# Grouped instance norm on one core: loads and stores on one queue, in a fixed order

## The chip, the cores and the metric

The kernel runs on one core of a Trainium2 chip. The metric is the device time of one execution in microseconds (us); lower is better. Engines are named as in the profile: PE (TensorE), DVE (VectorE), ACT (ScalarE), POOL (GpSimd) and SP (SyncE). The last computes nothing here; it issues DMAs. Sixteen DMA engines carry all transfers of the core.

## The reference

Each of 4 x 8 x 16 = 512 channels, an image of 256 x 256 float32 numbers, is normalized by its own mean and variance and scaled by one number per channel.

```python
def reference(x, gamma):               # x: (4, 8, 16, 256, 256), gamma: (8, 16), float32
    mu = x.mean(axis=(3, 4), keepdims=True)
    var = ((x - mu) ** 2).mean(axis=(3, 4), keepdims=True)
    x_norm = (x - mu) / np.sqrt(var + 1e-5)
    out = x_norm * gamma[None, :, :, None, None]
    return out.astype(np.float32)
```

The input has 134.22 MB and so has the output. Each number is read once and written once.

## The kernel before

The channels are worked off in 18 units, in order. A big unit is 32 channels, each spread over 4 partitions: a tile of 128 x 16384 float32, 8.39 MB. A small unit is 16 channels, each over 8 partitions: 128 x 8192, 4.19 MB. Units 0 and 1 are small, 2 to 15 are big, 16 and 17 are small again. Three slots in SBUF of 8.39 MB hold the data (`slots`, `SLOTS = 3`). Each big unit has a slot of its own, two small ones share one, and slots are taken in turn: units 0 and 1 in slot 0, unit 2 in slot 1, unit 3 in slot 2, unit 4 in slot 0, and so on, so that big unit u takes the slot of unit u-3. Units 16 and 17 are the halves of slot 0, after unit 13.

The instructions of each engine stand in the order in which the program writes them. For a unit u they are:

- DVE sums each partition's row (L128), ACT squares it and sums the squares (L130, in pieces of 8192 numbers, two for a big unit).
- PE adds the partial sums over the partitions of a channel (L138), which gives minus the mean and minus the mean square.
- DVE, ACT and DVE turn these into a scale per partition (L141 to L156).
- DVE subtracts the mean and multiplies by the scale, in place (L159).
- ACT issues the store of the unit (L163), so the store waits in ACT's order for L159.

The loads are all issued by SP (`load`, L70). Loads 0 to 3 go out at the start. Load 4 is written after store 1, and load u+3 after store u from there on. A load into a slot waits until the store that last read the slot has landed; this wait stands on SP, the store on ACT, and so the two kinds of transfer go through two queues.

```python
        nc.scalar.dma_start(out=rows(flat_o, u), in_=t)
        if u == 1:
            load(4)
        elif 2 <= u and u + 3 < U - 1:
            load(u + 3)
            if u + 3 == U - 2:
                load(U - 1)
```

Of the kernel before, what the change touches and what calls it, by code (L numbers as in the profile page):

```python
# [1 line left out]

# [4 lines left out]

F32 = mybir.dt.float32
U8 = mybir.dt.uint8
ALU = mybir.AluOpType  # L10
ACTF = mybir.ActivationFunctionType
AX = mybir.AxisListType


@with_exitstack
def kernel(
    ctx: ExitStack,
    tc: tile.TileContext,
    x: bass.AP,
    gamma: bass.AP,  # L20
    out: bass.AP,
):
    nc = tc.nc
    B, G, C, H, W = x.shape
    P = nc.NUM_PARTITIONS
    HW = H * W
    n_ch = B * G * C
    GC = G * C
    SLOTS = 3
    FS = HW // 8  # L30
    FB = HW // 4
    KB, KS = P // 4, P // 8


    flat_x = x.rearrange("b g c h w -> (b g c h w)")
    flat_o = out.rearrange("b g c h w -> (b g c h w)")

    data = ctx.enter_context(tc.tile_pool(name="data", bufs=1))
    singles = ctx.enter_context(tc.tile_pool(name="singles", bufs=1))
    psum = ctx.enter_context(tc.tile_pool(name="psum", bufs=4, space=bass.MemoryType.PSUM))  # L40
    ctx.enter_context(tc.manual_schedule())

    slots = [data.tile([P, FB], F32, name=f"xt{i}") for i in range(SLOTS)]

    units = []
    first = 0
    turn = 0

    def small(pair):
        nonlocal first, turn  # L50
        for h in range(2):
            units.append((first, 8, slots[turn % SLOTS][:, h * FS : (h + 1) * FS]))
            first += KS
        turn += 1

    small(0)
    while first < n_ch - KB:
        units.append((first, 4, slots[turn % SLOTS][:]))
        first += KB
        turn += 1  # L60
    small(1)
    U = len(units)

    def rows(flat, u):
        c0, s, _ = units[u]
        f = HW // s
        return flat[c0 * HW : c0 * HW + P * f].rearrange("(p f) -> p f", f=f)

    def load(u):
        nc.sync.dma_start(out=units[u][2], in_=rows(flat_x, u))  # L70

    g_kn = singles.tile([KB, GC // KB], F32, name="g_kn")
    for u in range(4):
        load(u)
    with nc.allow_non_contiguous_dma(reason="128 numbers"):
        nc.gpsimd.dma_start(out=g_kn[:], in_=gamma.rearrange("g c -> (g c)").rearrange("(n k) -> k n", k=KB))  # L76

    eps_t = singles.tile([P, 1], F32, name="eps_t")
    nc.gpsimd.memset(eps_t[:], 1e-5)
    root_eps = singles.tile([P, 1], F32, name="root_eps")  # L80
    nc.scalar.activation(out=root_eps[:], in_=eps_t[:], func=ACTF.Sqrt)  # L81

    def blocks(name, rows_, k, s, value, base):

        t = singles.tile([rows_, k, P // k], F32, name=name)
        nc.gpsimd.memset(t[:], value)
        nc.gpsimd.affine_select(  # L87
            out=t[:], in_=t[:], pattern=[[-s, k], [0, P // k]], compare_op=ALU.is_ge,
            fill=0.0, base=-base, channel_multiplier=1,
        )  # L90
        nc.gpsimd.affine_select(  # L91
            out=t[:], in_=t[:], pattern=[[s, k], [0, P // k]], compare_op=ALU.is_ge,
            fill=0.0, base=s - 1 + base, channel_multiplier=-1,
        )
        return t[:].rearrange("p k s -> p (k s)")

    navg = {8: blocks("navg8", P, KS, 8, -1.0 / HW, 0), 4: blocks("navg4", P, KB, 4, -1.0 / HW, 0)}
    pick = [
        blocks("pick8a", KB, KS, 1, 1.0, 0),
        blocks("pick8b", KB, KS, 1, 1.0, KS),  # L100
        blocks("pick4", KB, KB, 1, 1.0, 0),
    ]
    NB = GC // KB
    g_ps = psum.tile([P, 3, NB], F32, name="g_ps", bufs=1)
    g_col = singles.tile([P, 3, NB], F32, name="g_col")
    for i in range(3):
        nc.tensor.matmul(out=g_ps[:, i], lhsT=pick[i], rhs=g_kn[:], start=True, stop=True)  # L107
    nc.vector.tensor_copy(out=g_col[:], in_=g_ps[:])  # L108

    def gamma_of(u):  # L110
        c0, s, _ = units[u]
        n, rest = divmod(c0 % GC, KB)
        i = 2 if s == 4 else rest // KS
        return g_col[:, i, n : n + 1]

    junk = singles.tile([P, FS], U8, name="junk")
    st = singles.tile([P, U, 3], F32, name="st")
    nvar = singles.tile([P, U], F32, name="nvar")
    rest = singles.tile([P, U], F32, name="rest")
    std = singles.tile([P, U], F32, name="std")  # L120
    rstd = singles.tile([P, U], F32, name="rstd")
    scale = singles.tile([P, U], F32, name="scale")

    before = None
    for u in range(U):
        c0, s, t = units[u]
        parts = 8 // s
        nc.vector.reduce_sum(out=st[:, u, 0:1], in_=t, axis=AX.X)  # L128
        for h in range(parts):
            square = nc.scalar.activation(  # L130
                out=junk[:], in_=t[:, h * FS : (h + 1) * FS], func=ACTF.Square,
                accum_out=st[:, u, 1 + h : 2 + h],
            )
            if h == 0 and before is not None:
                tc.declare_no_dep(square.ins, before.ins, reason="junk, ordered by the root between")
            before = square
        ps = psum.tile([P, 3], F32, name="ps")
        nc.tensor.matmul(  # L138
            out=ps[:, : 1 + parts], lhsT=navg[s], rhs=st[:, u, : 1 + parts], start=True, stop=True,
        )  # L140
        nc.vector.tensor_scalar(  # L141
            out=nvar[:, u : u + 1], in0=ps[:, 0:1], scalar1=ps[:, 0:1],
            scalar2=ps[:, 1:2], op0=ALU.mult, op1=ALU.add,
        )
        bias = eps_t[:]
        if parts == 2:
            bias = rest[:, u : u + 1]
            nc.vector.tensor_scalar(  # L148
                out=bias, in0=ps[:, 2:3], scalar1=-1.0, scalar2=1e-5, op0=ALU.mult, op1=ALU.add,
            )  # L150
        nc.scalar.activation(  # L151
            out=std[:, u : u + 1], in_=nvar[:, u : u + 1], func=ACTF.Sqrt,
            bias=bias, scale=-1.0,
        )
        nc.vector.reciprocal(out=rstd[:, u : u + 1], in_=std[:, u : u + 1])  # L155
        nc.vector.tensor_mul(  # L156
            out=scale[:, u : u + 1], in0=rstd[:, u : u + 1], in1=gamma_of(u),
        )
        nc.vector.tensor_scalar(  # L159
            out=t, in0=t, scalar1=ps[:, 0:1], scalar2=scale[:, u : u + 1],  # L160
            op0=ALU.add, op1=ALU.mult,
        )
        nc.scalar.dma_start(out=rows(flat_o, u), in_=t)  # L163
        if u == 1:
            load(4)
        elif 2 <= u and u + 3 < U - 1:
            load(u + 3)
            if u + 3 == U - 2:
                load(U - 1)


# [1 line left out]
_INS = ['x', 'gamma']  # L173
_OUTS = [((4, 8, 16, 256, 256), 'float32')]


# [23 lines left out]
```

## Time and profile before

| what | value |
|---|---|
| median of 3 runs | 631.54 us (629.13 to 643.01) |
| the profiled execution's own time | 629.47 us |
| its span in the profile | 627.8 us |
| DVE busy | 429.4 us (68%) |
| ACT busy | 234.7 us (37%) |
| loads, q1 on SP | 134.22 MB, 49.8% of the 16 DMA engines |
| stores, q10 on ACT | 134.22 MB, 49.4% |
| HBM traffic over the span | 428 GB/s |
| big load, median from issue to landing | 43.5 us |
| big store, median from issue to landing | 44.7 us |

The span is the stretch of the device's time that the profile covers; the execution's own time has 1.7 us around it. "L128" is a line of the kernel file. A row of a group gives the engine, the operation, what it writes and reads, the count, its busy time with the mean of one in ns, and the idle time before it with what ended that. The share of a queue is the time that its packets took, as a part of the span of all 16 DMA engines.

### The profile page before, as it was taken

How to read it: one execution, taken by the hardware profiler on the slowest of the kernel's cores; microseconds unless marked ns; L12 is line 12 of the kernel's file. 1: busy time of each engine (PE TensorE's matmuls, PEld its weight loads, DVE VectorE, ACT ScalarE, POOL GpSimd, SP SyncE). 2: the span in 40 equal slices, each digit the busy share in tenths (PEclk: the TensorE clock that was granted, in tenths of full speed). 3: DMA queues.
4: the chain of work that ended last, by engine and by line, in shares of the span. 5: the costliest groups of instructions: out<-in, count | busy, mean ns of one | idle time of the engine just before them, and what ended most of it. 6: DMA issues, size and time to landing. Idle time of an engine off the chain costs nothing.

```text
span 627.8 us, 434 instructions
## 1 busy us (share of the span) xinstructions
PE 11.4 (2%) x42; PEld 10.4 (2%) x42; DVE 429.4 (68%) x105; ACT 234.7 (37%) x84; POOL 6.2 (1%) x21
## 2 busy tenths in 40 slices
PE   0000000000000000000000000000000000000000
PEld 0000000000000000000000000000000000000000
DVE  1978897097692956929569395792948839499780
ACT  2438190090621706217062260712608135081340
POOL 3000000000000000000000000000000000000000
DMA  9999999999999999999999999999999999999997
GB/s 363 438 401 451 411 457 418 451 418 451 418 447 422 447 422 447 414 451 418 451 418 451 413 455 413 455 405 464 401 468 401 468 401 468 401 447 420 449 411 303
DMA packets 5218, 268.45 MB, mean 428 GB/s; under 512 B 608, under 2 KB 608, under 8 KB 608
## 3 DMA queue, kind: packets, MB, share of 16 engines
q1 hardware_dynamic: 2592, 134.22, 49.8%
q10 hardware_dynamic: 2592, 134.22, 49.4%
q14 instruction: 2, 0.02, 0.0%
q0 software_dynamic: 32, 0.00, 0.0%
HBM read 134.22 MB, written 134.22 MB: 428 GB/s over the span
## 4 chain that ended last, share of the span: by engine, by line
DMA 63%; DVE 26%; another core or an unknown queue 7%; PE 1%; issue 0%; ACT 0%; SPq 0%
DMA xt<-in_x_dram 36%; DMA out_dram<-xt 28%; DVE st L128 16%; DVE xt L159 8%; PE ps L138 1%; ACT std L151 0%; DVE nvar L141 0%; SPq L70 0%; DVE rstd L155 0%; DVE scale L156 0%; DVE rest L148 0%
## 5 line engine op out<-in xcount | busy, mean ns | idle before, releaser
L128 DVE TENSOR_REDUCE st<-xt 128x1 f32<-128x16384 f32 (+1 forms) x18 | 275.8, 15323 | 151.5 <-DMA xt<-in_x_dram 151.5
L130 ACT ACTIVATE junk<-xt 128x8192 uint8<-128x8192 f32 x32 | 224.9, 7030 | 305.6 <-DMA xt<-in_x_dram 290.0
L159 DVE TENSOR_SCALAR xt<-xt,ps,scale 128x16384 f32<-128x16384 f32 (+1 forms) x18 | 141.7, 7870 | 0.7
L151 ACT ACTIVATE std<-nvar,rest 128x1 f32<-128x1 f32 x14 | 4.1, 294 | 57.0 <-DVE rest L148 57.0
L138 PE MATMUL ps<-st,navg 128*128 128x3 f32 (+1 forms) x36 | 10.0, 349 | 586.4 <-DVE st L128 586.4
L138 PEld LDWEIGHTS ps<-st,navg 128*128 128x128 f32 x36 | 9.0, 311 | 587.4 <-issue 587.4
L141 DVE TENSOR_SCALAR nvar<-ps 128x1 f32<-128x1 f32 x18 | 5.2, 287 | 13.4 <-PE ps L138 13.4
L108 DVE COPY g_col<-g_ps 128x12 f32<-128x12 f32 x1 | 0.2, 170 | 10.6 <-PE g_ps L107 10.6
L155 DVE RECIPROCAL rstd<-std 128x1 f32<-128x1 f32 x18 | 3.0, 164 | 6.5 <-ACT std L151 6.5
L130 ACT ACTIVATION_READ_ACCUMULATOR junk<-xt 128x1 f32 x32 | 6.0, 186 | 0.0
L151 ACT ACTIVATE std<-nvar,eps_t 128x1 f32<-128x1 f32 x4 | 1.2, 294 | 9.5 <-DVE nvar L141 9.5
L156 DVE TENSOR_TENSOR scale<-rstd,g_col 128x1 f32<-128x1 f32 x18 | 2.9, 159 | 0.6
L148 DVE TENSOR_SCALAR rest<-ps 128x1 f32<-128x1 f32 x14 | 2.1, 148 | 0.0
L81 ACT ACT_TABLE_LOAD x1 | 1.3, 1283 | 0.8 <-PEq L184 0.8
L87 POOL TENSOR_SCALAR_AFFINE_SELECT navg<-navg 128x128 f32<-128x128 f32 x2 | 0.9, 468 | 0.1
L91 POOL TENSOR_SCALAR_AFFINE_SELECT navg<-navg 128x128 f32<-128x128 f32 x2 | 0.9, 458 | 0.1
L107 PE MATMUL g_ps<-g_kn,pick8a 32*128 32x4 f32 x2 | 0.6, 344 | 9.1 <-DMA g_kn<-in_gamma_dram 9.1
L76 POOL DMA_DIRECT2D g_kn<-in_gamma_dram x1 | 0.7, 671 | 0.8 <-POOLq L184 0.8
L107 PEld LDWEIGHTS g_ps<-g_kn,pick8a 32*128 32x128 f32 x2 | 0.5, 305 | 9.1 <-issue 9.1
L107 PE MATMUL g_ps<-g_kn,pick 32*128 32x4 f32 x2 | 0.6, 349 | 0.0
L107 PE MATMUL g_ps<-g_kn,pick8b 32*128 32x4 f32 x2 | 0.6, 349 | 0.0
L107 PEld LDWEIGHTS g_ps<-g_kn,pick8b 32*128 32x128 f32 x2 | 0.5, 328 | 0.0
(17 smaller groups left out, 4.9 us busy)
## 6 DMA issues: line engine op xcount, KB each, us to landing
xt<-in_x_dram SPq DMA_DIRECT2D x4, 4096.0 KB, 26.8
out_dram<-xt ACTq DMA_DIRECT2D x4, 4096.0 KB, 28.4
xt<-in_x_dram SPq DMA_DIRECT2D x14, 43.5
out_dram<-xt ACTq DMA_DIRECT2D x14, 44.7
g_kn<-in_gamma_dram POOLq DMA_DIRECT2D x1, 0.5 KB, 7.6
```

What stands on the lines that cost most here:

```text
L81: nc.scalar.activation(out=root_eps[:], in_=eps_t[:], func=ACTF.Sqrt)
L87: nc.gpsimd.affine_select(out=t[:], in_=t[:], pattern=[[-s, k], [0, P // k]], compare_op=ALU.is_ge, fill=0.0, base=-base, channel_multipli ...
L107: nc.tensor.matmul(out=g_ps[:, i], lhsT=pick[i], rhs=g_kn[:], start=True, stop=True)
L128: nc.vector.reduce_sum(out=st[:, u, 0:1], in_=t, axis=AX.X)
L130: square = nc.scalar.activation(out=junk[:], in_=t[:, h * FS : (h + 1) * FS], func=ACTF.Square, accum_out=st[:, u, 1 + h : 2 + h],)
L138: nc.tensor.matmul(out=ps[:, : 1 + parts], lhsT=navg[s], rhs=st[:, u, : 1 + parts], start=True, stop=True,)
L141: nc.vector.tensor_scalar(out=nvar[:, u : u + 1], in0=ps[:, 0:1], scalar1=ps[:, 0:1], scalar2=ps[:, 1:2], op0=ALU.mult, op1=ALU.add,)
L148: nc.vector.tensor_scalar(out=bias, in0=ps[:, 2:3], scalar1=-1.0, scalar2=1e-5, op0=ALU.mult, op1=ALU.add,)
L151: nc.scalar.activation(out=std[:, u : u + 1], in_=nvar[:, u : u + 1], func=ACTF.Sqrt, bias=bias, scale=-1.0,)
L155: nc.vector.reciprocal(out=rstd[:, u : u + 1], in_=std[:, u : u + 1])
L156: nc.vector.tensor_mul(out=scale[:, u : u + 1], in0=rstd[:, u : u + 1], in1=gamma_of(u),)
L159: nc.vector.tensor_scalar(out=t, in0=t, scalar1=ps[:, 0:1], scalar2=scale[:, u : u + 1], op0=ALU.add, op1=ALU.mult,)
```

## The change

The store of unit u is issued by SP and not by ACT. Right behind it in SP's order stands the load of unit u+2, from u = 2 on; before, it was the load of unit u+3, on a queue that held loads alone. Load 4 is now written after store 2. Loads 16 and 17 both follow store 14; before they followed store 13. The slots stay as they are, so load u+2 goes into the slot that store u-1 read. Thus SP's order is loads 0, 1, 2, 3, stores 0, 1, 2, load 4, store 3, load 5, ..., store 14, loads 16 and 17, stores 15, 16, 17.

```diff
-        nc.scalar.dma_start(out=rows(flat_o, u), in_=t)
-        if u == 1:
-            load(4)
-        elif 2 <= u and u + 3 < U - 1:
-            load(u + 3)
-            if u + 3 == U - 2:
+        nc.sync.dma_start(out=rows(flat_o, u), in_=t)
+
+        if 2 <= u and u + 2 < U:
+            load(u + 2)
+            if u + 2 == U - 2:
                 load(U - 1)
```

## The prediction

> **What bounds the kernel now.** The page first: is any engine the limit, or the transfers?
>
> ```profile
> span 627.8 us, 434 instructions
> DMA  9999999999999999999999999999999999999997
> q1 hardware_dynamic: 2592, 134.22, 49.8%
> q10 hardware_dynamic: 2592, 134.22, 49.4%
> L128 DVE TENSOR_REDUCE st<-xt 128x1 f32<-128x16384 f32 (+1 forms) x18 | 275.8, 15323 | 151.5 <-DMA xt<-in_x_dram 151.5
> L159 DVE TENSOR_SCALAR xt<-xt,ps,scale 128x16384 f32<-128x16384 f32 (+1 forms) x18 | 141.7, 7870 | 0.7
> ```
>
> The 16 DMA engines are busy in every slice. The loads (q1, issued on SP) and the stores (q10, issued on ACT) take half of their time each, together 99.2% of the span. DVE, the busiest engine (429 us), waits 151.5 us for loads. So the transfers set the end, and a change can gain only by moving bytes faster or by closing gaps between them. The windows say how much that is (columns: stretch, length, busy time and count on PE, PEld, DVE, ACT, POOL, clock, DMA share, GB/s):
>
> ```profile
> 0.00:2.00 2.00, 0.00 (x0) 0.00 (x0) 0.00 (x0) 1.19 (x1) 0.85 (x5) 1.00 0.61 164
> 2.00:4.00 2.00, 0.00 (x0) 0.00 (x0) 0.00 (x0) 0.30 (x2) 1.77 (x7) 1.00 0.74 262
> 4.00:28.00 24.00, 1.96 (x8) 1.85 (x8) 13.10 (x6) 7.42 (x3) 3.55 (x10) 1.00 1.03 442
> 28.00:50.00 22.00, 0.56 (x2) 0.50 (x2) 14.70 (x7) 7.45 (x4) 0.00 (x0) 1.00 0.97 399
> 100.00:550.00 450.00, 6.14 (x22) 5.51 (x22) 300.72 (x67) 159.93 (x55) 0.00 (x0) 1.00 1.00 434
> 597.00:620.00 23.00, 0.56 (x2) 0.50 (x2) 13.85 (x5) 7.42 (x3) 0.00 (x0) 1.00 0.95 412
> 614.00:620.00 6.00, 0.00 (x0) 0.00 (x0) 0.00 (x0) 0.00 (x0) 0.00 (x0) 1.00 1.02 437
> 620.00:625.00 5.00, 0.00 (x0) 0.00 (x0) 0.00 (x0) 0.00 (x0) 0.00 (x0) 1.00 0.67 288
> 625.00:628.00 3.00, 0.00 (x0) 0.00 (x0) 0.00 (x0) 0.00 (x0) 0.00 (x0) 1.00 0.03 11
> ```
>
> For 450 us the engines are full and move 434 GB/s. All 268.44 MB at that rate take 618.5 us, so the span holds only 9.3 us of anything else. By stretch: the first 4 us move 0.85 MB instead of 1.74, 2.0 us lost; 28 to 50 runs at 399, 22 x (1 - 399/434) = 1.8 us; 597 to 620 at 412, 1.2 us; the last 8 us move 1.47 MB instead of 3.47, 4.6 us. That is 9.6, the whole gap to within rounding (short windows count whole packets, hence the 442).
>
> Last, the timeline of one big unit, which gives the compute between a load's landing and its store, and SP's own wait:
>
> ```profile
> 512.20 17.22 DVE L128 TENSOR_REDUCE st<-xt 128x1 f32<-128x16384 f32 x1 [10.75 <-DMA xt<-in_x_dram]
> ...
> 540.12 0.34 ACTq L163 DMA_DIRECT2D out_dram<-xt  x1
> 550.84 7.03 ACT L130 ACTIVATE junk<-xt 128x8192 uint8<-128x8192 f32 x1 [20.00 <-DMA xt<-in_x_dram]
> SPq L70 <- DMA out_dram<-xt: 537.4, 13, 79.6
> ```
>
> Landed at 512.20, store issued at 540.12: 27.9 us. The next lands at 550.84: a cycle of 38.64 us, which is one load and one store of 8.39 MB at 434 GB/s (2 x 19.3). DVE has 10.75 us over in each.
>
> **The change part by part.**
>
> *What leaves ACT.* 18 store issues of 0.34 us, 6.1 us, and with them ACT's wait for L159, which held up the squares of the next unit behind it. It costs nothing to lose and brings nothing: the squares (2 x 7.0 us for a big unit) hide under the 17.2 us sum on DVE. The issues now stand on SP, which computes nothing and spent 537.4 us waiting: 6.1 us hidden there.
>
> *What SP waits for, and who stands behind it.* SP takes its instructions in order, so load u+2 now stands behind the wait of store u for L159 of unit u. Before, load u+3 went out when store u had landed. I follow the ring as a line, each transfer after the last, at 19.3 us for a big one and 9.7 for a small one.
>
> Start: load 0 lands at 13.9 as before, loads 1, 2, 3 end at 23.6, 42.9, 62.2. Stores 0 and 1 are issued at 28.95 and 43.88 as before, but now stand behind load 3: they end at 71.9 and 81.6. Unit 2 starts on DVE at 43.9 (load landed, DVE just free) and its store is issued at 71.8, 10 us before its turn. Load 4 needs slot 0, free when store 1 has landed at about 82 to 84; its turn is at 100.9. Store 3 is ready at 99.7, its turn 120.2. Stores 0 and 1 are late by some 40 us, and only load 4 needs their slot, whose turn is later still.
>
> Middle: let load u land at t. The ring then carries store u-1 until t+19.3 and load u+1 until t+38.6. Store u is issued at t+27.9, 10.7 us before its turn, and load u+2 right behind it, its slot free since store u-1 ended at t+19.3. So the ring is never empty, and the cycle stays 38.6 us.
>
> End: with load 15 landing at T, store 14 ends at T+19.3, loads 16 and 17 at T+29.0 and T+38.6. Store 15 is ready at T+27.9 (turn T+38.6). DVE does units 16 and 17 in 15.0 us each (13.90 to 28.95 for unit 0), ready at T+44.0 and T+59.0, turns T+57.9 and T+67.6. The smallest margin of all is 8.6 us. The cover is this margin: without it every microsecond that a store is late would be one on the span, in each of 13 cycles.
>
> *One ring instead of two.* The engines no longer choose between a load and a store; long stretches only read, long ones only write. Loads alone on q1 run at 442 (4 to 28, three transfers back to back), stores alone on q10 at 437 (614 to 620). So following transfers of one direction cost nothing. New are changes of direction within one ring, which before doesn't show: loads 0 to 3 | stores 0 to 2 | load 4 | store 3 | load 5 ... store 14 | loads 16, 17 | stores 15 to 17, 14 changes to a store and 13 to a load. Lower bound 0 each: in the middle both queues share every engine at 434 GB/s and 1.00, so the engines change direction all the time for free. Upper bound 3.4 us each: load 0 took 13.1 us from issue to landing, of which its bytes are 9.7, an empty ring's whole latency. I take 0, since the middle has the same engines, the same rows and both directions; the other end would be 27 x 3.4 = 92 us.
>
> By the Trainium skill, "DMA: Bandwidth & Descriptors", section "Anatomy of one DMA", a DMA costs a fixed 2.0 us or so beside its bytes, mostly the receipt of the last write, heaviest where HBM is written. If that stood in the ring at each of the 27 changes, my estimate by that page is 54 us more, some 682 us in all. The trace does not agree for transfers of one direction (442 over the first loads); for a change of direction no run here shows it yet.
>
> *The ends.* The 2.0 us at the start stay. The 1.8 us in 28 to 50 fall where store 0 begins beside the loads; in one ring it comes later and alone, gain 0 to 1.8, I take half, 0.9. The 1.2 us in 597 to 620 fall where the last store was issued only at 612.67, when its queue was nearly dry; now it stands 8.6 us early: gain 1.2. The 4.6 us of the last stretch stay (bounds: 2.5 lost at least, the empty 625 to 628).
>
> **Sum.** 618.5 + 2.0 + 0.9 + 4.6 = 626.0 us of span. The profiled run took 629.47 for a span of 627.8, 1.7 us around it, so 627.7 against 629.47. The median shown is 631.5, 2.1 above the profiled run; I add 0.8 for such scatter and say 628.5.
>
> **The rivals.**
>
> *Forecast, 0.72:* full ring, own range 624.5 (all bounds of the ends taken as gains: 618.5 + 2.0 + 2.5 + 1.7) to 633.
>
> *Not one line after all, 0.06:* the ring lets a load pass a waiting store, or stores still share the engines with loads. Then the middle is what it was: 629.5. For it: a load and a store that are both issued could run together. Against: loads 1 to 3, all issued by 1.7 us, came one after the other.
>
> *Changes of direction empty the engines, 0.10:* slower side. Price 1.2 us each, from the 2.0 us lost at the start less the 0.8 before the first issue: 27 x 1.2 = 32, so 660. It decides from 0.47 us each (12.6 us, 2%). For it: nothing else fills an engine now, where the second queue did. Against: the free alternation in the middle.
>
> *Each direction alone is slower than the mix, 0.05:* 597 to 620 (stores) at 412, and loads alone from 2 to 26 at 423, if they are taken as they stand: 134.2/0.412 + 134.2/0.423 = 643 instead of 618.5, so 653. Against: 442 and 437, without the ramp and the late last store.
>
> *The load waits for the store just ahead, 0.05:* if load u+2 were held for store u itself and not for store u-1 (a shared counter), the ring would run empty once in each of 13 cycles at up to 3.4 us: 44 us, 672. Against: slot u+2 is slot u-1 with three slots.
>
> *Faster by over 2%, 0.02:* that is below 617 us, under the 618.5 that the bytes need at the only rate seen.
>
> **Chances.** 2% is about what a measurement of this kernel can tell from no change. Faster 0.02, same 0.72 + 0.06 = 0.78, slower 0.10 + 0.05 + 0.05 = 0.20. The range runs from 624.5 to 642, half a microsecond a change, which leaves out most of the three slow cases.
>
> **What would show it.** Right: one queue with 268 MB and a share near 99%; 434 GB/s in every slice but the first and last; a cycle of 38.6 us with some 10.7 us of DVE idle; loads landing about 49 us after issue (t+27.9 to t+77.3) and stores about 30 (t+27.9 to t+57.9); the last store issued some 18 us before the end. Wrong: a DMA share below 0.97 in the middle (changes of direction, or a dry ring: then a store is issued after the load before it has landed), or a share of 1.00 with less than 425 GB/s (slower direction).

## The result, and the profile after

The changed kernel takes 647.44 us (median of 4 runs, 646.47 to 648.18) against 631.56 us for the kernel before (4 runs). The ratio is 1.0264, with a 95% interval from 1.0229 to 1.0299: slower by 2.6%. The ratios here and below compare fast runs alone: one run of the kernel before (643.01 us), and further down one of e2 (668.40 us), were slow and are left out. The forecast was no change (628.5 us, range 624.5 to 642).

First the page of the changed kernel: its span, DVE, what the DMA engines moved, and the rows of the issues.

```profile
span 646.3 us, 415 instructions
DMA  8999999999999999999999999999999999999956
GB/s 353 462 418 412 428 450 446 410 442 446 418 430 450 438 406 446 447 406 446 443 414 442 438 430 418 450 434 422 442 446 402 450 446 402 446 422 442 428 245 260
q1 hardware_dynamic: 5328, 272.63, 97.9%
HBM read 138.41 MB, written 134.22 MB: 422 GB/s over the span
L128 DVE TENSOR_REDUCE st<-xt 128x1 f32<-128x16384 f32 (+1 forms) x18 | 275.8, 15322 | 172.7 <-DMA xt<-in_x_dram 172.7
xt<-in_x_dram SPq DMA_DIRECT2D x5, 4096.0 KB, 29.1
```

Two things stand out. The last two slices fall to 245 and 260 GB/s, while all others stay where they were. And HBM read 138.41 MB where the input has 134.22: 4.19 MB more, one small unit. The row of small loads says the same, with a count of 5 where there are four small units. So one unit is loaded twice. The end of the timeline shows which (start and length in us, engine, line, operation; in brackets the idle time before and what ended it):

```profile
540.48 0.85 SPq L70 DMA_DIRECT2D xt<-in_x_dram  x2
...
578.85 0.34 SPq L163 DMA_DIRECT2D out_dram<-xt  x1
...
589.99 0.33 SPq L70 DMA_DIRECT2D xt<-in_x_dram  x1
...
594.96 0.34 SPq L163 DMA_DIRECT2D out_dram<-xt  x1
619.08 8.69 DVE L128 TENSOR_REDUCE st<-xt 128x1 f32<-128x8192 f32 x1 [24.16 <-DMA xt<-in_x_dram]
...
634.13 0.34 SPq L163 DMA_DIRECT2D out_dram<-xt  x1
```

The waits of SP's queue (us in total, times, longest) show what the added load waits for:

```profile
SPq L70 <- DMA xt<-in_x_dram: 10.8, 1, 10.8
```

Loads 16 and 17 go out at 540.48, behind store 14. Store 15 follows at 578.85, and behind it comes one more load. It is that of unit 17 again: the new condition `u + 2 < U` is also true at u = 15 (17 < 18), and unit 17 has already been loaded by the inner `load(U - 1)` at u = 14. The condition before was `u + 3 < U - 1`, and stopped in time. **The description of the change above is therefore incomplete**: SP's order ends with store 15, load 17 once more, stores 16 and 17. The second load waits 10.8 us on SP until the first has landed (589.99), queues behind store 15, and lands at 619.08. DVE was done with unit 16 at 594.9 and waits 24.16 us for a unit that had already been there. After that, 15.05 us of compute stand before the last store (634.13), and nothing is left to transfer but the rest of store 16.

The windows of the changed kernel (stretch, length, busy time of five engines, clock, DMA share, GB/s):

```profile
100.00:550.00 450.00, 6.13 (x22) 5.50 (x22) 293.85 (x66) 159.93 (x55) 0.00 (x0) 1.00 1.00 434
600.00:620.00 20.00, 0.00 (x0) 0.00 (x0) 0.92 (x1) 0.92 (x1) 0.00 (x0) 1.00 1.00 434
620.00:634.00 14.00, 0.56 (x2) 0.50 (x2) 12.82 (x5) 6.50 (x3) 0.00 (x0) 1.00 0.23 101
634.00:647.00 13.00, 0.00 (x0) 0.00 (x0) 0.11 (x1) 0.00 (x0) 0.00 (x0) 1.00 0.75 323
```

The middle, with all its changes of direction on one queue, runs at the same 434 GB/s as before with two. The loss stands in 620 to 634: 14 x (1 - 101/434) = 10.7 us of nearly empty ring (the ring is the line of transfers that have been issued and not yet moved), beside the 9.7 us that 4.19 MB take at 434 GB/s.

### The profile page after: what moved, and what is told of

Read it like the earlier page. It is cut to its first block, busy times and chain, and to the rows that moved or that the text cites. A ratio compares the mean times of both kernels' runs of the same rounds, so it can differ in the third digit from the quotient of the medians.

```text
span 646.3 us, 415 instructions
## 1 busy us (share of the span) xinstructions
PE 11.5 (2%) x42; PEld 10.4 (2%) x42; DVE 429.3 (66%) x105; ACT 234.6 (36%) x84; POOL 6.2 (1%) x21
## 3 DMA queue, kind: packets, MB, share of 16 engines
q1 hardware_dynamic: 5328, 272.63, 97.9%
HBM read 138.41 MB, written 134.22 MB: 422 GB/s over the span
## 4 chain that ended last, share of the span: by engine, by line
DMA 65%; DVE 31%; PE 1%; issue 1%; ACT 0%; SPq 0%
DMA xt<-in_x_dram 59%; DVE st L128 20%; DVE xt L159 10%; DMA out_dram<-xt 6%; PE ps L138 1%; ACT std L151 0%; DVE nvar L141 0%; SPq L163 0%; DVE rstd L155 0%; DVE scale L156 0%; SPq L70 0%; DVE rest L148 0%
## 6 DMA issues: line engine op xcount, KB each, us to landing
xt<-in_x_dram SPq DMA_DIRECT2D x14, 49.4
out_dram<-xt SPq DMA_DIRECT2D x14, 30.4
```

## The experiments

The theory (A): the second load of unit 17 is the whole loss, 9.7 us of bytes and some 10.7 us of empty ring at the end, and one queue costs nothing. Its rival (B): one queue costs by itself.

**e1: one queue, unit 17 loaded once.**

```diff
-        if 2 <= u and u + 2 < U:
+        if 2 <= u and u + 2 < U - 1:
```

> One queue and the changed order, but with the guard u + 2 < U - 1, so that unit 17 is loaded once. Theory A (all of the loss is the second load of unit 17, which the condition u + 2 < U lets through at u = 15): 268 MB on one queue, 434 GB/s throughout, span 646.3 - 9.7 (bytes) - 10.7 (empty ring at the end) = 626, time 627 to 630, within 1% of before. Theory B (one queue costs by itself, through changes of direction or late stores): the time stays above 640.

Measured: 630.67 us (12 runs) against 630.94 (17 runs), ratio 0.9999, interval 0.9982 to 1.0015. From its page:

```profile
span 628.4 us, 414 instructions
q1 hardware_dynamic: 5184, 268.44, 99.0%
```

Three of its windows, used below:

```profile
28.00:50.00 22.00, 0.56 (x2) 0.50 (x2) 20.82 (x7) 10.29 (x5) 0.00 (x0) 1.00 1.00 432
50.00:100.00 50.00, 1.12 (x4) 1.01 (x4) 47.03 (x12) 21.97 (x9) 0.00 (x0) 1.00 0.98 421
620.00:629.00 9.00, 0.00 (x0) 0.00 (x0) 0.00 (x0) 0.00 (x0) 0.00 (x0) 1.00 0.31 135
```

One changed token undoes the whole loss: theory B falls. The queue, the order and the later loads together make no difference of more than 0.2% either way. The time is 0.7 us above the 627 to 630 expected and the span 2.4 us above the 626 (the ends, below).

**e2: the kernel before, two queues, with the second load.**

```diff
-        elif 2 <= u and u + 3 < U - 1:
+        elif 2 <= u and u + 3 < U:
```

> The kernel before with its two queues, but the guard u + 3 < U, so that unit 17 is loaded a second time, behind the issue of store 14. Theory A: the second load goes out when the first has landed (597.6 before) and shares the engines with stores 15 and 16, lands near 618, 15 us of compute, the last store 12 us alone: time 645 to 650, as slow as the changed kernel though it has two queues. Theory B: near 632 to 640, the bytes at most (9.7 us).

Measured: 655.63 us, ratio 1.0395 (1.0367 to 1.0422). So the same slip costs two queues even more, and more than the 645 to 650 that A expected. From its timeline:

```profile
626.46 8.69 DVE L128 TENSOR_REDUCE st<-xt 128x1 f32<-128x8192 f32 x1 [31.32 <-DMA xt<-in_x_dram]
```

And the window from 620 us to the last store:

```profile
620.00:642.00 22.00, 0.56 (x2) 0.50 (x2) 13.85 (x5) 7.42 (x3) 0.00 (x0) 1.00 0.14 58
```

Unit 17 is there at 626.46, not at the 618 that I had worked out. The first load landed some 5 us later than I took it from the kernel before (the second went out at about 602), and the second took some 24 us beside stores 15 and 16. The engines then stand nearly empty for 22 x (1 - 58/434) = 19.1 us. 19.1 + 9.7 is 28.8, more than the 25.9 us by which its span exceeds that before. Most of the rest comes back in the last stretch: 642 to 653.7 moves 350 GB/s over 12 us and loses 2.0 us, the last stretch of the kernel before lost 4.6.

**e3: both loads of unit 17 together, ahead of store 15.** This and the next take the two parts of the loss apart.

```diff
-        if 2 <= u and u + 2 < U:
+        if 2 <= u and u + 2 < U - 1:
             load(u + 2)
             if u + 2 == U - 2:
                 load(U - 1)
+                load(U - 1)
```

> One queue; unit 17 is loaded twice, but the second load stands right behind the first, ahead of store 15. Theory A splits the loss into bytes (9.7 us) and an empty ring at the end (10.7): here the bytes stay, the second load waits for the first to land (ring empty 1.2 to 3.4 us), and unit 17 is ready under store 15, so the end is full: time 638 to 641. Rival (the bytes are hidden, the late landing is everything): 628 to 631. Rival (a second load costs all of it wherever it stands): 646 to 648.

Measured: 644.07 us, ratio 1.0221 (1.0195 to 1.0248), more than the 638 to 641 expected. The end is full, as expected: 427 GB/s from 600 to 640. But the wait of the second load for the first costs more than the 3.4 us that I had taken from load 0 (windows of 10 us, and the last 6 us of the first in steps of 2):

```profile
580.00:590.00 10.00, 0.56 (x2) 0.50 (x2) 8.90 (x3) 7.29 (x3) 0.00 (x0) 1.00 0.50 216
590.00:600.00 10.00, 0.00 (x0) 0.00 (x0) 4.83 (x3) 0.00 (x0) 0.00 (x0) 1.00 1.01 390
584.00:586.00 2.00, 0.00 (x0) 0.00 (x0) 2.00 (x1) 2.00 (x1) 0.00 (x0) 1.00 0.42 180
586.00:588.00 2.00, 0.00 (x0) 0.00 (x0) 2.00 (x1) 1.00 (x2) 0.00 (x0) 1.00 0.15 66
588.00:590.00 2.00, 0.56 (x2) 0.50 (x2) 0.90 (x3) 0.29 (x1) 0.00 (x0) 1.00 0.04 16
```

10 x (1 - 216/434) + 10 x (1 - 390/434) = 6.0 us are lost there, not 1.2 to 3.4. The second load waits on SP until the first has landed, and store 15 stands behind it in SP's order: its unit was done at 578.80 (569.98 + 8.82), and it is issued only at 589.93. So nothing follows the first load 17 in the ring. The rate falls long before that load has landed: the 16 DMA engines are busy to 0.42 at 584 to 586, to 0.15 in the next 2 us and to 0.04 in the last 2, so most engines had finished their part of the load well before the last one did. 9.7 + 6.0 = 15.7, of which 14.2 show in the span (642.6 against 628.4).

**e4: unit 17 loaded once, but behind store 15.**

```diff
             load(u + 2)
-            if u + 2 == U - 2:
-                load(U - 1)
```

> One queue; unit 17 is loaded once, but only behind store 15, where the changed kernel has its second load. Bytes as before. Theory A: unit 17 lands near 609, its store goes out near 624.5 with the ring empty for some 8 to 11 us, time 636 to 640. Rival (the bytes of the second load are everything): 627 to 630.

Measured: 639.85 us, ratio 1.0151 (1.0128 to 1.0174), as A expected. With no byte more, 9.4 us of span are lost, half of what the changed kernel loses. They stand in two places:

```profile
570.00:590.00 20.00, 0.56 (x2) 0.50 (x2) 17.77 (x6) 7.42 (x3) 0.00 (x0) 1.00 0.86 372
615.00:627.00 12.00, 0.56 (x2) 0.50 (x2) 9.35 (x5) 2.91 (x3) 0.00 (x0) 1.00 0.41 175
```

7.2 us at the end, while unit 17 is computed, and 2.9 us near 580: without load 17 there, only load 16 stood in the ring when store 15 was issued at 578.00, and it landed at 579.02. Both rivals, bytes alone and lateness alone, fall: e3 and e4 each show one part of the loss without most of the other.

**e5: the order of the kernel before on one queue.** Load u+3 stands behind store u, whose slot it needs.

```diff
-        nc.scalar.dma_start(out=rows(flat_o, u), in_=t)
+        nc.sync.dma_start(out=rows(flat_o, u), in_=t)
```

> The order of the kernel before (load u+3 behind store u, whose slot it takes), but with the stores on SP's queue too. It measures the rival by which a load waits for the store just ahead of it. Theory A: each of the 13 loads 4 to 16 holds SP until store u has landed, so the ring runs empty once in each cycle; at 3.4 us (an empty ring's latency in the first load) that is 44 us, 675; at 4.5 us (the 14.2 us that the two loads together cost above the single load, less 9.7 for the bytes) 59 us, 690. Rival (the ring doesn't run empty): 631.

Measured: 676.14 us, ratio 1.0724 (1.0689 to 1.0759), by the first of A's two prices. This is what one queue costs with the other order. A cycle from its timeline:

```profile
166.55 8.82 DVE L159 TENSOR_SCALAR xt<-xt,ps,scale 128x16384 f32<-128x16384 f32 x1
...
209.62 0.34 SPq L70 DMA_DIRECT2D xt<-in_x_dram  x1
210.01 0.42 SPq L163 DMA_DIRECT2D out_dram<-xt  x1
...
251.90 0.34 SPq L70 DMA_DIRECT2D xt<-in_x_dram  x1
```

SP's waits:

```profile
SPq L70 <- DMA out_dram<-xt: 537.1, 13, 42.0
```

From load to load the cycle is 42.28 us (209.62 to 251.90), 3.6 more than 38.64. A store that was ready at 175.37 (166.55 + 8.82) is issued only at 210.01: for 34.6 us it stood on SP behind a load that waited for the store before it. When that store has landed, the ring is empty. 13 such waits make (674.0 - 628.4)/13 = 3.5 us each, close to the 3.4 us taken from the first load.

**e6 and e7: more changes of direction.** In e1, the big stores of units 2 to 13 and the loads behind them are cut into n = 2 or 4 column pieces, which go out in turn. A part of the edit (`both` is true for these units, `w` is the range of columns, `v` is u + 2):

```diff
+            nc.sync.dma_start(out=rows(flat_o, u)[:, w], in_=t[:, w])
+            if both:
+                nc.sync.dma_start(out=units[v][2][:, w], in_=rows(flat_x, v)[:, w])
```

> One queue, unit 17 loaded once; where a big store is followed by a big load (units 2 to 13), both are cut into two column halves and go out in turn: half a store, half a load, half a store, half a load. 27 + 12 x 2 = 51 changes of direction instead of 27, 60 transfers instead of 36, the same bytes. Theory A (a change of direction in a full ring is free): 630 to 633. Rival (each costs 0.47 us or more): 642 or more. By the page's fixed 2.0 us for each transfer, if it stood in the ring: some 678.

> The same with four quarters: 27 + 12 x 6 = 99 changes of direction, 108 transfers, 16 KB instead of 64 KB a row and transfer. Theory A: 630 to 635. Rival (0.47 us or more a change): 664 or more. It bounds the price of one change to the measured difference divided by 72.

Measured: 631.22 us for halves (ratio 0.9999, 0.9977 to 1.0021) and 632.07 for quarters (1.0017, 0.9994 to 1.0040). The middle of the kernel with quarters:

```profile
100.00:550.00 450.00, 6.14 (x22) 5.51 (x22) 293.82 (x66) 167.07 (x57) 0.00 (x0) 1.00 1.01 431
```

72 more changes and 72 more transfers than in e1 cost 632.07 - 630.67 = 1.4 us, 0.02 us each; the 48 more than in e6 cost 0.85 us, the same price. By the window it is 450 x (1 - 431/434) = 3.1 us, 0.04 each. A change of direction in a full ring costs some hundredths of a microsecond at most.

## Why the prediction was wrong

**The step that failed** is the list of the ring at the end: "loads 16, 17, stores 15 to 17", and with it "One queue with 268 MB". I carried the guard of the old condition over to the new one and didn't evaluate `u + 2 < U` at u = 15. From there the bytes (268.44 instead of 272.63 MB), the turn of store 17 and the end of the sum were wrong. The sum said 626.0 us of span; the profiled one was 646.3. The two omitted terms are 9.7 us of bytes and 10.7 us of empty ring, less about 3 us that the last stretch gives back (634 to 646.3 loses 2.6 us, the same stretch of e1, 620 to 628.4, loses 5.6). That is 17.4, against 17.9 between the spans of the changed kernel and e1. The other 2.4 us between the sum and the profile are the ends (below). None of the rivals had this mechanism.

**What held.** Without the slip (e1), the time is that before, as forecast: the forecast of 628.5 stands against 630.67. Step by step: the middle keeps 434 GB/s on one queue. In the changed kernel a big load lands 49.4 us after its issue and a big store 30.4 (forecast 49 and 30), DVE is idle some 10.7 to 11.8 us in each cycle from unit 5 on (10.7), and in e1 the last store goes out at 608.82, 19.6 us before the end (18). The margin of about 10 us for each store holds; e4 shows what it is worth, since there a store that comes with too little in the ring ahead of it costs 2.9 us at once.

**Changes of direction** (0 to 3.4 us each, taken as 0): e6 and e7 show 0.02 to 0.04 for those in the middle. The fixed 2.0 us of the Trainium skill, "DMA: Bandwidth & Descriptors", section "Anatomy of one DMA", which that section gives for DMAs issued from GpSimd, do not add up in a full ring: for the 72 more transfers of e7 they would be, as an estimate, 144 us, and the runs show 1.4. Where the ring runs empty, e5 shows 3.5 us a time, more than that section's figure.

**The load that waits for the store just ahead** was the rival at 672; e5 makes that mechanism real and gives 676.14. Its price was nearly right (45.6 us of span for the 44); the slots of the changed kernel avoid it, as argued.

**The ends** were mis-sized. The sum kept 0.9 us for the dip where store 0 begins beside the loads. In e1 the 28 to 50 stretch does recover (432 GB/s, 0.1 us lost), but 50 to 100 falls to 421 and loses 1.5 us, most of it in 50 to 62 (385 GB/s), where the loads end and the first store begins. So the dip moved instead of going away; why there is one was not tried. The sum took the 1.2 us of 597 to 620 as regained; in e1, 550 to 620 still runs at 429 and loses 0.8. It took 4.6 us for the last stretch; in e1 it is 5.6. Together 0.7 + 0.8 + 1.0 = 2.5 us, which is the difference between e1's 628.4 and the sum's 626.0 to within rounding.

**Two smaller slips** carry no weight: the terms of the lower bound add up to 624.7 and not to 624.5, and the trace before shows the last of loads 0 to 3 issued from 2.2 us on, not by 1.7.

## What to carry to other kernels

Evaluate a loop's guard at its last values, and compare the bytes moved with the bytes that the computation needs, before any reading of waits: here the one line "HBM read 138.41 MB" shows that a unit is read twice, which is 9.7 us of the loss, and leads to the rest. When the DMA engines are full, as in this kernel, it matters little which queue a transfer goes through or in what order it goes, as long as something always stands behind it in the ring. What counts on a shared queue is what an issuing engine waits for with other transfers behind it: waiting for a store one unit back costs nothing (e1), waiting for the one just issued costs 3.5 us each time (e5).

## What the runs showed of the hardware

Moving the stores from ACT's queue to SP's costs nothing with one order (0.9999) and 7.2% with another (1.0724). The Trainium skill, "DMA: Bandwidth & Descriptors", section "Issuing engines are not separate DMA queues", says that issuing from several engines only saves the time to initiate a DMA. e1 agrees; e5 doesn't, since a second issuing engine there also keeps a ready store from standing 34.6 us behind a waiting load.

What a wait for a landing costs was not one figure: e5's waits for a big store lose 3.5 us each, near the 3.4 of load 0, but e3's wait for the small load 17 loses 6.0 us, 5.0 of them before the load has landed. Why e3's is dearer was not tried.
